# HGRN2 scores on one core: short distances and the diagonal through quarters of the array's columns

## The chip, the cores and the metric

The kernel runs on one core of a Trainium2 chip. The metric is device time of one execution in microseconds (us), as the median of several runs; a profile of one execution shows where it went.

## The reference, cut to what matters

One decoder layer over 1024 tokens of width 1024, in float32: a mixer with two parallel groups (HGRN2, a gated linear recurrence with 4 heads of 128, and a gated short convolution), then a gated MLP. Only the recurrence matters here. For each head, in chunks of tokens:

```python
b = jnp.cumsum(gc, axis=-2)                            # gc = log of the forget gate f
diff = b[..., :, None, :] - b[..., None, :, :]
decay = jnp.exp(jnp.where(causal[:, :, None], diff, -jnp.inf))
scores = jnp.einsum('bhtk,bhsk,bhtsk->bhts', qc, kc, decay)
o = (jnp.einsum('bhts,bhsv->bhtv', scores, vc)
     + jnp.einsum('bhtk,bhkv->bhtv', qc * jnp.exp(b), state))
state = exp(b_last) * state + jnp.einsum('bhsk,bhsv->bhkv', kc * jnp.exp(b_last - b), vc)
```

The decay differs for every channel k, so a score of two tokens is a sum over channels of q, k and the product of the gates between them.

## The kernel before

The tokens are worked in two halves (hf 0 and 1) of 512, each of 4 chunks of 128 (C). Projections, the output projection and the MLP are done as three float32r matmuls for each product (high by high, high by low, low by high): L181 to L183 and L186 to L188, tiles p_q, p_f, p_i, p_g (queries, gates, values, output gates), p_gc, p_ch, p_gb (convolution), p_wo (output projection) and later those of the MLP. They are TensorE's main stream, with 512 moving columns each.

Scores are plain float32 matmuls and are built by distance. UW holds, for 8 pairs of head and chunk (4 heads, 2 chunks of each parity), keys and queries of even and odd chunks as four blocks K, Q, K, Q. F holds the gates. For a chunk, a score of tokens whose positions first part at a block of h tokens belongs to level h (LEVELS, 1 to 64), and the diagonal stands for itself.

- products and diag: kq is the elementwise product of keys and queries, split into kqh and kql; a matmul with ones_r sums it over channels in all 128 rows of sd, and a masked copy (m_diag) puts the diagonal into S.
- level(li): 8 pairs by 2 halves of the chunk's tokens (`tile_position=(0, w * W)`, W = 64), a stationary operand of 64 columns of lhs and 64 moving columns of UW. Then two updates multiply the gates into UW (L389 the left factors, L391 the right ones, so that the next level finds the products over twice the distance), L393 combines the gates in F, and masked copies (m_lev, L399) or, for h = 64, plain copies (L403) put the scores sl into S.
- prepare(li): ScalarE gathers the left factors into lhs, which has one buffer (L371).
- The scores of odd chunks come out transposed: S is copied to odd and even (L443, L444), odd is transposed (so), and copied back.
- chunk_steps: for each chunk output (kt, o), state (st) and finish (mt), with the state carried from chunk to chunk.

These steps wait in a queue named fill. The projections call tick() at set places (the tuples named rate, rates and conv_rates), and each tick takes the next step from the queue, so a step's matmuls stand as a burst between projection matmuls. The steps of the residual and its norm (scale, residual, normalize) go through the same queue in the second half. Weights arrive by SyncE's queue into three buffers and are split on ScalarE (L119) and VectorE (L120).

Of the kernel before, what the change touches and what calls it, by code (L numbers as in the profile page):

```python
# [17 lines left out]
P = 128  # L18
# [5 lines left out]
H = 4  # L24
# [14 lines left out]
G = 2  # L39
GH = G * H  # L40
W = C // 2
N_MASK = C + W * (len(LEVELS) - 1)


@with_exitstack
def decoder_kernel(ctx: ExitStack, tc: tile.TileContext, x, xT, w_sq, w_cv, w_out, w_up, w_dn,
# [24 lines left out]
    m_lev = zp.tile([P, len(LEVELS) - 1, 2, W // 2, GH], U8, name="m_lev")  # L71
# [6 lines left out]
    ones_r = zp.tile([P, P], F32R, name="ones_r")  # L78
    nc.vector.tensor_copy(ones_r[:], ones[:])
# [159 lines left out]
    S = zt("S", (P, 2, C, GH))  # L239
# [56 lines left out]

    def evac_f(hf, pss, rb):
# [3 lines left out]
        kv = UW.rearrange("p (x s) (g j) t -> p x s g j t", x=2, j=H)[:, :, 0]  # L301
        for j, ps in enumerate(pss):
            t = cv(f"tf{hf}_{j}")
            nc.vector.tensor_tensor(t[:], ps[:], rb[:], ALU.mult)
            tv = t.rearrange("p (g x t) -> p x g t", g=2, x=2)
            fj, kj = Fv[:, :, :, j, :], kv[:, :, :, j, :]
            nc.scalar.activation(fj, tv, AF.Sigmoid)
            nc.scalar.activation(kj, tv, AF.Sigmoid, scale=-1.0)
            nc.vector.tensor_scalar(fj, fj, oml[:, j : j + 1], lb[:, j : j + 1], ALU.mult, ALU.add)
            nc.vector.tensor_scalar(kj, kj, oml[:, j : j + 1], None, ALU.mult)  # L310
        return F, UW

    def evac_q(hf, pss, rb, UW):
        nc.scalar.activation(warm, UW[:, 2, 7, 0:1], AF.Silu)
        qv = UW.rearrange("p (x s) (g j) t -> p x s g j t", x=2, j=H)[:, :, 1]
# [23 lines left out]
    def score_steps(hf, F, UW):  # L339
        kq = {}  # L340

        def products(xi, g):
            gs = slice(g * H, (g + 1) * H)
            p = cv(f"kq{hf}_{xi}_{g}", shape=(P, C, H))
            nc.vector.tensor_tensor(
                p.rearrange("p t i -> p i t"), UW[:, 2 * xi, gs, :], UW[:, 2 * xi + 1, gs, :], ALU.mult)
# [3 lines left out]
            kq[xi, g] = hi, lo  # L350

        def diag(xi, g):
            gs = slice(g * H, (g + 1) * H)
            hi, lo = kq[xi, g]
            ps = aux(f"sd{hf}_{xi}_{g}", (P, C, H))
            nc.tensor.matmul(ps[:], ones_r[:], hi[:], start=True, stop=False)
            nc.tensor.matmul(ps[:], ones_r[:], lo[:], start=False, stop=True)
            nc.vector.copy_predicated(S[:, xi, :, gs], m_diag[:].unsqueeze(2).to_broadcast([P, C, H]), ps[:])
            if xi == 1:
                q = UW.rearrange("p (x s) g t -> p x s g t", x=2)[:, :, 1, gs, :]  # L360
                nc.vector.tensor_tensor(q, q, F[:, :, gs, :], ALU.mult)

        def view(t, width, offset, *dims):
            return bass.AP(tensor=t[:].tensor, offset=offset, ap=[[width, P], *[list(d) for d in dims]])
# [3 lines left out]
        def prepare(li):  # L368
            h = LEVELS[li]
            lhss[li] = zt("lhs", (P, GH, C), name=f"lhs{hf}_{li}")  # L370
            nc.scalar.copy(lhss[li].rearrange("p i (b two h) -> p (i b) two h", two=2, h=h),  # L371
                           view(UW, 4 * X, 0, (2 * h, X // (2 * h)), (3 * X + h, 2), (1, h)))

        def level(li):

            h = LEVELS[li]
            n = X // (2 * h)
            ps = aux(f"sl{hf}_{li}", (P, 2, W // 2, GH) if h < W else (P, W, GH))
            lhs = lhss.pop(li)
            halves = [slice(w * W, (w + 1) * W) for w in range(2)]  # L380
            for i in range(GH):
                for w, ws in enumerate(halves):
                    if h < W:
                        rhs = view(UW, 4 * X, X + i * C + w * W + h, (X - h, 2), (2 * h, W // (2 * h)), (1, h))
                    else:
                        rhs = view(UW, 4 * X, X + i * C + (h, X)[w], (1, h))
                    nc.tensor.matmul(ps[ws, ..., i], lhs[:, i, ws], rhs, start=True, stop=True, tile_position=(0, w * W))
            u = view(UW, 4 * X, 0, (3 * X + h, 2), (2 * h, n), (1, h))
            nc.vector.tensor_tensor(u, u, view(F, 2 * X, h, (X - h, 2), (2 * h, n), (0, h)), ALU.mult)  # L389
            w = view(UW, 4 * X, X + h, (X - h, 2), (2 * h, n), (1, h))  # L390
            nc.vector.tensor_tensor(w, w, view(F, 2 * X, 0, (X + h, 2), (2 * h, n), (0, h)), ALU.mult)  # L391
            left = view(F, 2 * X, 0, (X, 2), (2 * h, n))
            nc.vector.tensor_tensor(left, left, view(F, 2 * X, h, (X, 2), (2 * h, n)), ALU.mult)  # L393
            for w, ws in enumerate(halves):
                if h < W:
                    sv = S[ws]
                    to = bass.AP(tensor=sv.tensor, offset=sv.offset + (w * W + h) * GH,
                                 ap=[list(sv.ap[0]), [X - h * GH, 2], [2 * h * GH, W // (2 * h)], [1, h * GH]])
                    nc.vector.copy_predicated(  # L399
                        to, m_lev[ws, li].rearrange("p x (b h) i -> p x b (h i)", h=h),  # L400
                        ps[ws].rearrange("p x (b h) i -> p x b (h i)", h=h))
                else:
                    nc.scalar.copy(S[ws, w, (1 - w) * W : (2 - w) * W], ps[ws])  # L403
# [7 lines left out]
        xg = [(xi, g) for g in range(2) for xi in range(2)]  # L411

        steps = [chain((products, *xg[0]))] + [chain()] * (2 * hf)
        for i in range(4):
            steps.append(chain((diag, *xg[i]), *([(products, *xg[i + 1])] if i < 3 else []),
                               *([(prepare, 0)] if i == 3 else [])))
        for li in range(len(LEVELS)):
            steps.append(chain((level, li), *([(prepare, li + 1)] if li + 1 < len(LEVELS) else [])))
        return steps
# [4 lines left out]
    def chunk_steps(hf, F, UW, v, gg, ma):  # L424
        ma_hi, ma_lo = ma
        shared = {}

        def make(c):
# [4 lines left out]
            K, Q = UW[:, 2 * xi], UW[:, 2 * xi + 1]  # L433
# [3 lines left out]
            def scores():  # L437

                if c == 1:
                    shared["even"] = zt("lhs", (P, GH, C), name=f"even{hf}")  # L440
                    for gi in range(G):
                        shared[gi] = cv(f"odd{hf}_{gi}", shape=(P, H, C))
                        nc.scalar.copy(shared[gi].rearrange("p i t -> p t i"), S[:, 1, :, gi * H : (gi + 1) * H])  # L443
                    nc.scalar.copy(shared["even"].rearrange("p i t -> p t i"), S[:, 0])  # L444
                ps = aux(f"so{n}", (P, H, C))
                for j in range(H):
                    nc.tensor.transpose(ps[:, j, :], shared[g][:, j], ident[:])
                odd = S[:, 1].rearrange("p t i -> p (t i)").rearrange("p (i t) -> p i t", t=C)
                shared["odd"] = odd
                nc.scalar.copy(odd[:, g * H : (g + 1) * H], ps[:])  # L450

            def output():
# [8 lines left out]
                for _, ph, js in hs:  # L461
                    if not first:
                        nc.tensor.matmul(po[:, js], Q[:, ph, :], st[0][:, js], start=True, stop=False)
                    nc.tensor.matmul(po[:, js], shared[("even", "odd")[xi]][:, ph, :], v[c][:, js], start=first, stop=True)
# [87 lines left out]
    def out_proj(hf, mix, gain, hooks=None):  # L552
# [46 lines left out]
        for nh in range(2):  # L599
            if nh and hf:  # L600
                for c in range(NC_H):
# [3 lines left out]
                            hooks=hooks if nh == 0 else None, rate=(2, 2, 1, 1) if hf + nh == 0 else 1)  # L605
# [82 lines left out]
    nc.sync.dma_start(mf[:], masks_d)  # L688
    nc.gpsimd.tensor_copy(m_diag[:], mf[:, :C])
    mv = mf[:, C:].rearrange("p (l x n) -> p l x n", x=2, n=W // 2)  # L690
    for l in range(len(LEVELS) - 1):
# [15 lines left out]
    mix_a = mixers(0, act_a, F0, UW0, rb0, rq0, r0, ma_tiles(0), (1, (1, 1, 1, 2)), (1, 1, 1, 2, 1, 2, 1, 2, 1, 2, 2, 2),  # L707
# [14 lines left out]
    mix_b = mixers(1, act_b, F1, UW1, rb1, rq1, r1, ma_tiles(1), (1, 2), (1, 2, 1, 1, 2, 1, 1, 2, 1, 1, 2, 1))  # L722
# [447 lines left out]
def _masks():  # L1170

    p = np.arange(C)[:, None]
    t = p // W * W + np.arange(W)
    m = [np.eye(C)]
    for h in LEVELS[:-1]:
        same = p // (2 * h) == t // (2 * h)
        left_p, left_t = (p // h) % 2 == 0, (t[0] // h) % 2 == 0
# [53 lines left out]
```

## Time and profile before

| | |
|---|---|
| median of 3 runs | 1100.7 us (1100.54 to 1100.79) |
| the profiled execution | 1099.83 us, its span 1098.0 us |
| level bursts (tile sl) | 14, of 32 records each, from 85.4 to 306.7 us |
| diagonal (tile sd) | 8 times 2 matmuls, from 61.6 to 257.7 us |
| transposes of odd scores (so) | from 126.9 to 345.8 us |

Times in rows are microseconds from the start of the span, or nanoseconds where a row gives min, median and max. PE is TensorE, DVE VectorE, ACT ScalarE. A matmul's record overlaps the next one's, so the spacing of starts tells what one costs in a stream. Each float32 matmul stands as two records; "x32" counts records.

### The profile page before, as it was taken

What the parts mean: (1) busy time and instruction counts of PE and PEld (TensorE: products, weight loads), DVE (VectorE), ACT (ScalarE), POOL (GpSimd) and SP (SyncE); (2) the same over time, 40 slices, a digit from 0 to 9 for tenths busy, and PEclk for the clock granted to TensorE, in tenths of its full rate; (3) what the DMA queues carried; (4) which work ended last, traced back from release to release, by engine and by line L of the source; (5) the groups of instructions that cost most, each with busy time, mean ns of one, the idle gap of its engine ahead of it and who ended that gap; (6) DMA issues with size and microseconds to landing.
All of it is one profiled execution on the core that took longest, in us unless ns stands there. A gap on an engine that the chain in (4) does not pass through costs nothing.

```text
span 1098.0 us, 13874 instructions
## 1 busy us (share of the span) xinstructions
PE 1087.5 (99%) x5312; PEld 900.7 (82%) x5312; DVE 821.5 (75%) x1150; ACT 521.3 (47%) x765; POOL 13.5 (1%) x24
## 2 busy tenths in 40 slices
PE   9999999999999999999999999999999999999996
PEld 7888888888788888888888888888888888888885
DVE  7567977466965675487789888889888767855886
ACT  5543545433454336466445454544454444544541
POOL 2000000000000001000000000000000000000000
PEclk9999999999999999999999999999999999999999
DMA  8522223432352356175243433343332479776632
GB/s 295 190 96 77 81 74 121 138 96 81 116 169 97 106 171 222 66 237 187 85 163 115 153 115 144 125 163 138 130 134 73 155 259 407 304 260 228 209 109 104
DMA packets 56018, 170.14 MB, mean 155 GB/s; under 512 B 5640, under 2 KB 6160, under 8 KB 53008
## 3 DMA queue, kind: packets, MB, share of 16 engines
q1 hardware_dynamic: 54736, 165.24, 43.2%
q0 software_dynamic: 912, 3.67, 1.0%
q8 instruction: 41, 0.67, 0.2%
q10 hardware_dynamic: 304, 0.35, 0.1%
q14 instruction: 25, 0.20, 0.1%
HBM read 133.84 MB, written 35.39 MB: 154 GB/s over the span
## 4 chain that ended last, share of the span: by engine, by line
PE 96%; DVE 3%; issue 0%; ACT 0%; DMA 0%; DVEq 0%; SPq 0%; ACTq 0%
PE pG L181 7%; PE pG L183 7%; PE pG L182 7%; PE pV L181 4%; PE pV L183 4%; PE pV L182 4%; PE pX L188 3%; PE pX L186 3%; PE pX L187 3%; PE pY L186 3%; PE pY L187 3%; PE pY L188 3%; PE p_wo L186 3%; PE p_wo L188 2%; PE p_wo L187 2%; PE pA L183 2%
## 5 line engine op out<-in xcount | busy, mean ns | idle before, releaser
L120 DVE TENSOR_TENSOR ls<-s,hs 128x1024 fp32r<-128x1024 f32 (+1 forms) x40 | 45.2, 1130 | 46.3 <-ACT hs L119 44.4
L119 ACT CAST hs<-s 128x1024 fp32r<-128x1024 f32 (+1 forms) x40 | 39.1, 976 | 78.7 <-PE pY L187 29.9
L796 DVE TENSOR_TENSOR l_t<-t,h_t 128x1536 fp32r<-128x1536 f32 x22 | 38.6, 1755 | 32.6 <-ACT h_t L795 32.6
L795 ACT CAST h_t<-t 128x1536 fp32r<-128x1536 f32 x22 | 32.6, 1484 | 55.2 <-PE pG L182 55.2
L895 ACT ACTIVATE g<-g 128x1024 f32<-128x1024 f32 x22 | 23.4, 1062 | 64.8 <-DVE g L883 64.8
L188 PE MATMUL pY<-hw,ls 128*128 128x512 f32 x132 | 51.4, 390 | 0.0
L187 PE MATMUL pY<-lw,hs 128*128 128x512 f32 x132 | 51.4, 389 | 0.0
L186 PE MATMUL pY<-hw,hs 128*128 128x512 f32 x132 | 51.3, 390 | 0.0
L186 PE MATMUL pX<-hw,hs 128*128 128x512 f32 x116 | 45.2, 390 | 0.0
L187 PE MATMUL pX<-lw,hs 128*128 128x512 f32 x116 | 45.2, 390 | 0.0
L188 PE MATMUL pX<-hw,ls 128*128 128x512 f32 x116 | 45.2, 390 | 0.0
L881 ACT ACTIVATE g<-pG,vec 128x1024 f32<-128x1024 f32 x22 | 24.5, 1114 | 29.0 <-PE pG L183 29.0
L182 PE MATMUL pG<-ulo,h_x 128*128 128x512 f32 x96 | 37.4, 390 | 0.0
L183 PE MATMUL pG<-uhi,l_x 128*128 128x512 f32 x96 | 37.4, 390 | 0.0
L181 PE MATMUL pG<-uhi,h_x 128*128 128x512 f32 x96 | 37.4, 389 | 0.0
L882 DVE SCALAR_TENSOR_TENSOR g<-pG,vec,g 128x1023 f32<-128x1023 f32 x22 | 28.2, 1280 | 8.8 <-ACT g L881 8.3
L181 PE MATMUL pG<-c4h,h_b 128*128 128x512 f32 x88 | 34.4, 390 | 0.0
L182 PE MATMUL pG<-c4l,h_b 128*128 128x512 f32 x88 | 34.3, 390 | 0.0
L183 PE MATMUL pG<-c4h,l_b 128*128 128x512 f32 x88 | 34.3, 390 | 0.0
L181 PE MATMUL pV<-c3h,h_b 128*128 128x512 f32 x88 | 34.3, 390 | 0.0
L183 PE MATMUL pV<-c1h,l_t 128*128 128x512 f32 x88 | 34.3, 390 | 0.0
L181 PE MATMUL pG<-c2h,h_t 128*128 128x512 f32 x88 | 34.3, 390 | 0.0
(366 smaller groups left out, 3362.8 us busy)
## 6 DMA issues: line engine op xcount, KB each, us to landing
w<-w_up SPq DMA_DIRECT2D x21, 1024.0 KB, 4.8
b<-w_dn SPq DMA_DIRECT2D x35, 512.0 KB, 7.8
s<-s_d SPq DMA_DIRECT2D x33, 512.0 KB, 4.7
s_d<-g SPq DMA_DIRECT2D x22, 512.0 KB, 2.7
s_d<-S SPq DMA_DIRECT2D x11, 768.0 KB, 3.5
r_wo<-w_out SPq DMA_DIRECT2D x16, 512.0 KB, 3.5
ah_w<-w_up SPq DMA_DIRECT2D x10, 512.0 KB, 4.5
f_d<-ah_f SPq DMA_DIRECT2D x9, 512.0 KB, 3.0
```

The costliest lines, as they stand in the source:

```text
L119: nc.scalar.copy(hi, src)
L120: nc.vector.tensor_tensor(lo, src, hi.bitcast(F32), ALU.subtract)
L181: nc.tensor.matmul(ps, whi, ahi, start=first, stop=False, skip_group_check=more)
L182: nc.tensor.matmul(ps, whi, alo, start=False, stop=False, skip_group_check=more)
L183: return nc.tensor.matmul(ps, wlo, ahi, start=False, stop=last, skip_group_check=more)
L186: nc.tensor.matmul(ps, ahi, whi, start=first, stop=False, skip_group_check=more)
L187: nc.tensor.matmul(ps, ahi, wlo, start=False, stop=False, skip_group_check=more)
L188: return nc.tensor.matmul(ps, alo, whi, start=False, stop=last, skip_group_check=more)
L795: m = nc.scalar.copy(hi[:], src)
L796: casts[name] = m.ins, nc.vector.tensor_tensor(lo[:], src, hi[:].bitcast(F32), ALU.subtract).ins
L881: nc.scalar.mul(a[:], c, wc[2])
L882: nc.vector.scalar_tensor_tensor(a[:, 1:], c[:, : T - 1], wc[1], a[:, 1:], ALU.mult, ALU.add)
```

## The change

Levels 1 to 32 work on quarters of 32 tokens: 4 matmuls for each of the 8 pairs, with 32 stationary and 32 moving columns, at column positions 0, 32, 64 and 96. Levels 1 to 16 and the diagonal are masked into a small tile near, whose token index counts within 32 tokens, with 5 masks instead of 6; 8 plain copies (put_near) bring it into S, and levels 32 and 64 are copied into S from sl. The diagonal is summed by plain float32 matmuls with a stationary operand of 32 columns of ones, in four column positions, so the split into kqh and kql is gone; products and diag work on 8 pairs at a time. S is kept as pair by token, so the copies odd and even are gone. The blocks of UW lie as K, Q, Q, K, and prepare(li + 1) is called inside level(li), between its two updates. There are two steps fewer in each half's queue; the rates at some places are changed with it.

```diff
-G = 2
-GH = G * H
-W = C // 2
+GH = 2 * H
+W = 32
+LOW = sum(h < W for h in LEVELS)
...
-    ones_r = zp.tile([P, P], F32R, name="ones_r")
-    nc.vector.tensor_copy(ones_r[:], ones[:])
+    near = zp.tile([P, 2, W, GH], F32, name="near")
+    nc.gpsimd.memset(near[:], 0.0)
...
-    S = zt("S", (P, 2, C, GH))
+    S = zt("S", (P, 2, 8, C))
...
+    K_AT, Q_AT = (0, 3), (2, 1)
...
-            nc.scalar.activation(qv[:, :, :, j, :], t.rearrange("p (g x t) -> p x g t", g=2, x=2), AF.Silu)
+            for xi in range(2):
+                nc.scalar.activation(
+                    qv[:, Q_AT[xi], :, j, :], t.rearrange("p (g x t) -> p x g t", g=2, x=2)[:, xi], AF.Silu)
...
-            hi = cv(f"kqh{hf}_{xi}_{g}", F32R, (P, C, H))
-            lo = cv(f"kql{hf}_{xi}_{g}", F32R, (P, C, H))
-            split(p[:], hi[:], lo[:])
...
-            nc.tensor.matmul(ps[:], ones_r[:], hi[:], start=True, stop=False)
-            nc.tensor.matmul(ps[:], ones_r[:], lo[:], start=False, stop=True)
-            nc.vector.copy_predicated(S[:, xi, :, gs], m_diag[:].unsqueeze(2).to_broadcast([P, C, H]), ps[:])
...
+        def diag(xi):
+            ps = aux(f"sd{hf}_{xi}", (P, GH, W))
+            for g in range(2):
+                for q in range(C // W):
+                    ws = slice(q * W, (q + 1) * W)
+                    nc.tensor.matmul(ps[ws, g * H : (g + 1) * H], ones[:, :W], kq[xi, g][:, :, ws], start=True, stop=True,
+                                     tile_position=(0, q * W))
+            nc.vector.copy_predicated(near[:, xi], m_diag[:, :W].unsqueeze(2).to_broadcast([P, W, GH]),
+                                      ps.rearrange("p i t -> p t i"))
...
-                           view(UW, 4 * X, 0, (2 * h, X // (2 * h)), (3 * X + h, 2), (1, h)))
+                           view(UW, 4 * X, 0, (2 * h, X // (2 * h)), (X + h, 2), (1, h)))
...
-            halves = [slice(w * W, (w + 1) * W) for w in range(2)]
+            low, wide = h < W, max(h, W)
+            parts = [slice(t, t + wide) for t in range(0, C, wide)]
             for i in range(GH):
-                for w, ws in enumerate(halves):
+                for q, ws in enumerate(parts):
...
-                    nc.tensor.matmul(ps[ws, ..., i], lhs[:, i, ws], rhs, start=True, stop=True, tile_position=(0, w * W))
-            u = view(UW, 4 * X, 0, (3 * X + h, 2), (2 * h, n), (1, h))
+                    nc.tensor.matmul(ps[ws, ..., i], lhs[:, i, ws], rhs, start=True, stop=True, tile_position=(0, ws.start))
+            u = view(UW, 4 * X, 0, (X + h, 2), (2 * h, n), (1, h))
             nc.vector.tensor_tensor(u, u, view(F, 2 * X, h, (X - h, 2), (2 * h, n), (0, h)), ALU.mult)
-            w = view(UW, 4 * X, X + h, (X - h, 2), (2 * h, n), (1, h))
+            if li + 1 < len(LEVELS):
+                prepare(li + 1)
+            w = view(UW, 4 * X, 2 * X + h, (X - h, 2), (2 * h, n), (1, h))
...
+        def put_near(xi):
+            for t in range(0, C, W):
+                ws = slice(t, t + W)
+                nc.scalar.copy(S[ws, xi, :, ws], near[ws, xi].rearrange("p t i -> p i t"))
...
-                        nc.scalar.copy(shared[gi].rearrange("p i t -> p t i"), S[:, 1, :, gi * H : (gi + 1) * H])
-                    nc.scalar.copy(shared["even"].rearrange("p i t -> p t i"), S[:, 0])
...
-                            hooks=hooks if nh == 0 else None, rate=(2, 2, 1, 1) if hf + nh == 0 else 1)
+                            hooks=hooks if nh == 0 else None, rate=(2, 1, 1, 1) if hf + nh == 0 else 1)
...
-    mix_a = mixers(0, act_a, F0, UW0, rb0, rq0, r0, ma_tiles(0), (1, (1, 1, 1, 2)), (1, 1, 1, 2, 1, 2, 1, 2, 1, 2, 2, 2),
+    mix_a = mixers(0, act_a, F0, UW0, rb0, rq0, r0, ma_tiles(0), (1, 1), (1, 1, 1, 2, 1, 1, 2, 1, 1, 2, 2, 1),
...
-    mix_b = mixers(1, act_b, F1, UW1, rb1, rq1, r1, ma_tiles(1), (1, 2), (1, 2, 1, 1, 2, 1, 1, 2, 1, 1, 2, 1))
+    mix_b = mixers(1, act_b, F1, UW1, rb1, rq1, r1, ma_tiles(1), ((1, 1, 1, 2), 2), (1, 2, 1, 1, 2, 1, 1, 2, 1, 1, 2, 1))
```

Two places of TensorE's order show what moves. The first is the burst of level 0 in the first half; sl is its result, p_g the projection of output gates, p_i that of values. Before:

```order
L186 MATMUL p_g_3_705<-h_g_1_744,hi_3_206 128x512
L187 MATMUL p_g_3_705<-l_g_1_745,hi_3_206 128x512
L188 MATMUL p_g_3_705<-h_g_1_744,lo_3_207 128x512
L387 MATMUL sl_0_773<-UW_392,lhs_0_741 64x64 x16
L186 MATMUL p_g_0_702<-h_g_2_798,hi_4_236 128x512
L187 MATMUL p_g_0_702<-l_g_2_799,hi_4_236 128x512
L188 MATMUL p_g_0_702<-h_g_2_798,lo_4_237 128x512
L186 MATMUL p_g_0_702<-h_g_2_798,hi_5_257 128x512
```

and in the changed kernel:

```order
L186 MATMUL p_i_3_539<-h_i_3_663,hi_7_308 128x512
L187 MATMUL p_i_3_539<-l_i_3_664,hi_7_308 128x512
L188 MATMUL p_i_3_539<-h_i_3_663,lo_7_309 128x512
L391 MATMUL sl_0_692<-UW_392,lhs_0_660 32x32 x32
L186 MATMUL p_g_0_739<-h_g_0_744,hi_0_135 128x512
L187 MATMUL p_g_0_739<-l_g_0_745,hi_0_135 128x512
L188 MATMUL p_g_0_739<-h_g_0_744,lo_0_136 128x512
```

The burst has 32 matmuls of 32 columns instead of 16 of 64, and it stands two ticks earlier, between the last matmul of the values and the first of the gates.

The second place is level 3 of the second half, behind the output projection of the first half (p_wo). Before:

```order
L186 MATMUL p_i_0_2454<-h_i_1_2513,hi_3_1710 128x512
L387 MATMUL sl_3_2488<-UW_1886,lhs_3_2438 64x64 x9
L186 MATMUL p_i_3_2457<-h_i_0_2459,hi_0_1692 128x512
L187 MATMUL p_i_3_2457<-l_i_0_2460,hi_0_1692 128x512
L188 MATMUL p_i_3_2457<-h_i_0_2459,lo_0_1693 128x512
L186 MATMUL p_i_3_2457<-h_i_0_2459,hi_1_1698 128x512
L187 MATMUL p_i_3_2457<-l_i_0_2460,hi_1_1698 128x512
L188 MATMUL p_i_3_2457<-h_i_0_2459,lo_1_1699 128x512
L387 MATMUL sl_3_2488<-UW_1886,lhs_3_2438 64x64 x7
L187 MATMUL p_i_0_2454<-l_i_1_2514,hi_3_1710 128x512
```

and in the changed kernel:

```order
L186 MATMUL p_wo_1_3_2321<-h_wo_1_3_2532,mah_534 128x512
L187 MATMUL p_wo_1_3_2321<-l_wo_1_3_2533,mah_534 128x512
L188 MATMUL p_wo_1_3_2321<-h_wo_1_3_2532,mal_535 128x512
L391 MATMUL sl_3_2563<-UW_1972,lhs_3_2526 32x32 x32
L186 MATMUL p_i_0_2616<-h_i_0_2621,hi_0_1778 128x512
L187 MATMUL p_i_0_2616<-l_i_0_2622,hi_0_1778 128x512
L188 MATMUL p_i_0_2616<-h_i_0_2621,lo_0_1779 128x512
L186 MATMUL p_i_0_2616<-h_i_0_2621,hi_1_1784 128x512
```

The burst stood in two pieces, 9 and 7 matmuls, among the projection of values with a part of another of its rows drawn in between; now it is one piece of 32, directly behind the output projection.

More of the change, by code (lines that the diff above doesn't have):

```diff
@@ L38 @@
 V_N = V_FCONV + 3 * 2 * NF
-G = 2
-GH = G * H
-W = C // 2
-N_MASK = C + W * (len(LEVELS) - 1)
+GH = 2 * H
+W = 32
+LOW = sum(h < W for h in LEVELS)
+N_MASK = W * (1 + LOW)
 @with_exitstack
@@ L70, in decoder_kernel @@
     m_diag = zp.tile([P, C], U8, name="m_diag")
-    m_lev = zp.tile([P, len(LEVELS) - 1, 2, W // 2, GH], U8, name="m_lev")
+    m_lev = zp.tile([P, LOW, 2, W // 2, GH], U8, name="m_lev")
     conv_halo = zp.tile([P, 4, 2], F32, name="conv_halo")
@@ L409, in chain @@
             return run
[L411 to L419, printed above, removed]
+        steps = [chain((products, 0))] + [chain()] * (2 * hf)
+        steps += [chain((diag, 0), (products, 1)), chain((diag, 1), (prepare, 0))]
+        return steps + [chain((step, li)) for li in range(len(LEVELS))]
     st = [None]
@@ L437, in scores @@
             def scores():
[L439 to L444, printed above, removed]
-                ps = aux(f"so{n}", (P, H, C))
[L446 to L450, printed above, removed]
+                ps = aux(f"so{n}", (P, H, C))
+                for j, ph, _ in hs:
+                    nc.tensor.transpose(ps[:, j, :], S[:, 1, ph, :], ident[:])
+                nc.scalar.copy(S[:, 1, g * H : (g + 1) * H, :], ps[:])
             def output():
@@ L463, in output @@
                         nc.tensor.matmul(po[:, js], Q[:, ph, :], st[0][:, js], start=True, stop=False)
-                    nc.tensor.matmul(po[:, js], shared[("even", "odd")[xi]][:, ph, :], v[c][:, js], start=first, stop=True)
+                    nc.tensor.matmul(po[:, js], S[:, xi, ph, :], v[c][:, js], start=first, stop=True)
                 ssq = small(f"sso{n}")
@@ L687, in decoder_kernel @@
     mf = xslot("mf")
[L688 to L691, printed above, removed]
+    nc.sync.dma_start(mf[:, :N_MASK], masks_d)
+    nc.gpsimd.tensor_copy(m_diag[:, :W], mf[:, :W])
+    mv = mf[:, W:N_MASK].rearrange("p (l x n) -> p l x n", x=2, n=W // 2)
+    for l in range(LOW):
         nc.gpsimd.tensor_copy(m_lev[:, l], mv[:, l].unsqueeze(3).to_broadcast([P, 2, W // 2, GH]))
```

78 lines of the change are left out of this document (39 added, 39 removed).

## The prediction

> **What bounds the kernel now.** I read the page's engine totals first, then the chain that ended last, the order of time on TensorE around the instructions that the change touches, and last the groups and waits of their tiles.
>
> ```profile
> span 1098.0 us, 13874 instructions
> PE 1087.5 (99%) x5312; PEld 900.7 (82%) x5312; DVE 821.5 (75%) x1150; ACT 521.3 (47%) x765; POOL 13.5 (1%) x24
> PEclk9999999999999999999999999999999999999999
> PE 96%; DVE 3%; issue 0%; ACT 0%; DMA 0%; DVEq 0%; SPq 0%; ACTq 0%
> ```
>
> TensorE is busy 99% of the span at the full granted clock, and 96% of the chain that ended last is TensorE. So a change pays only by what it takes from TensorE's own row of matmuls, or from the few tenths of a microsecond where that row has a gap. The question is what one burst of score matmuls costs there. Rows in order of time, of TensorE alone (start us, us, then the operation):
>
> ```profile
> 85.07 0.39 PE L188 MATMUL p_g<-h_g,lo 128*128 128x512 f32 x1
> 85.39 1.16 PE L387 MATMUL sl<-UW,lhs 128*64 128x64 f32 x32
> 86.48 0.50 PE L186 MATMUL p_g<-h_g,hi 128*128 128x512 f32 x1
> 86.82 0.40 PE L187 MATMUL p_g<-l_g,hi 128*128 128x512 f32 x1
> 87.05 0.39 PE L188 MATMUL p_g<-h_g,lo 128*128 128x512 f32 x1
> 126.89 0.39 PE L183 MATMUL p_gc<-hi,l_gc 128*128 128x512 f32 x1
> 127.12 1.09 PE L447 MATMUL so<-ident,odd 128*128 128x128 f32 x8
> 127.97 0.48 PE L181 MATMUL p_ch<-hi,h_ch 128*128 128x512 f32 x1
> ```
>
> Projection matmuls start 0.23 us apart (86.82 to 87.05). Every float32 matmul of the scores stands as two records (16 in the program, x32 here). One level of distances delays the projection by 86.82 - 85.07 = 1.75 us less two normal steps, 1.75 - 0.45 = **1.30 us**. There are 14 such bursts (7 levels, two halves), some 18 us, all on the path.
>
> A second place shows gaps, in the second half of the tokens, where a burst waits and the next comes in two pieces:
>
> ```profile
> 276.92 0.39 PE L188 MATMUL p_wo<-h_wo,mal 128*128 128x512 f32 x1
> 277.66 1.15 PE L387 MATMUL sl<-UW,lhs 128*64 128x64 f32 x32 [0.35 <-ACT lhs L371]
> 283.65 0.39 PE L186 MATMUL p_i<-h_i,hi 128*128 128x512 f32 x1
> 284.13 0.80 PE L387 MATMUL sl<-UW,lhs 128*64 128x64 f32 x18
> 285.34 0.50 PE L186 MATMUL p_i<-h_i,hi 128*128 128x512 f32 x1 [0.42 <-DVE m_o L550]
> 286.92 0.68 PE L387 MATMUL sl<-UW,lhs 128*64 128x64 f32 x14
> ```
>
> **The change part by part.** *Levels 1 to 32 through quarters of the columns.* A level had 8 heads x 2 halves of the columns; it gets 8 heads x 4 quarters, each with 32 moving columns instead of 64. Twelve bursts change; the two of level 64 keep their form.
>
> What is one step worth? In the piece of 18 records one half works through 10 and the other through 8; the piece of 14 has 8 at most on a half, the whole burst of 32 has 16. So (1.16 - 0.68) / (16 - 8) = **0.060 us for one step**, and both halves take that step together: 32 records of 0.060 one after the other would be 1.9 us. A record of the same kind with 128 moving columns takes (127.97 - 127.12) / 8 = 0.106 us alone. A straight line through 64 columns (0.060) and 128 columns (0.106) gives 0.037 us for 32 columns. Strict proportion to 64 columns gives 0.030 us. No shrinking at all gives 0.060. And quarters that can't be fed together give more (the rival below). I take 0.037, since both of its rows are float32 records of this kind and the second half joined the first at no cost: the last two steps of the piece of 18 are one half alone, and its length (0.80 against 0.68 for two steps fewer) has the same 0.060 per step. What isn't steps in a burst, 1.30 - 16 x 0.060 = 0.34 us, is entry and exit (85.07 to 85.39 is 0.32, not 0.23; 86.48 to 86.82 is 0.34), and stays.
>
> So a level goes from 1.30 to 0.34 + 16 x 0.037 = 0.93 us; 12 x 0.37 = **-4.4 us** (-5.8 at 0.030, 0 at 0.060).
>
> The Trainium skill has a rule against this: "TensorE: Matmul & The Clock Gate", section "Wait — 56ns, not 53.3ns?", says that matmuls of one kind don't start closer than about 25 ns however few their columns (with 32 columns 25 ns, against 13.3 ns of array time), and "TensorEngine Tiling (Array Packing)", section "Instruction Overhead", says not to take the tiling from a dimension that is already small. If each record here pays that floor twice, an estimate from that page is 0.050 us a step; the level term is then -1.9 us and the time 1097.0 us. No row of before has fewer than 64 moving columns on half an array, so the trace doesn't decide it.
>
> *Diagonal.* Before, each of 8 products went through two full-array matmuls:
>
> ```profile
> 61.34 0.40 PE L188 MATMUL p_i<-h_i,lo 128*128 128x512 f32 x1
> 61.58 0.40 PE L356 MATMUL sd<-kqh,ones_r 128*128 128x512 f32 x1
> 61.81 0.39 PE L357 MATMUL sd<-kql,ones_r 128*128 128x512 f32 x1
> 62.04 0.40 PE L186 MATMUL p_i<-h_i,hi 128*128 128x512 f32 x1
> ```
>
> That is 62.04 - 61.58 = 0.46 us each with no entry or exit cost, 3.7 us in all. Now there are 4 bursts of 8 float32 matmuls (16 records) in four quarters, so 4 steps of 128 columns at 0.106, plus 0.34 for entry and exit: 0.76 each, 3.1 us in all: **-0.6 us**. If the quarters don't overlap, 16 x 0.106 + 0.34 = 2.0 us each, +4.4.
>
> *Copies of the left factor, and the regrouping.* Keys and queries of the two parities lay as K, Q, K, Q; now they lie as K, Q, Q, K, so that the left factors of all levels are one half of the tile and the right factors the other; and the copy for the next level is issued ahead of the second update instead of behind it. What it is worth is read from the waits of the copies (tile lhs; engine awaited, us, times):
>
> ```profile
> L371 ACT COPY lhs<-UW x14: 1037/1054/1527, 67.1 to 302.7; 128x1024 f32<-128x1024 f32 x14
>   DVE UW L391: 21.2, 7
>   ACT lhs L371: 4.1, 10
> L389 DVE TENSOR_TENSOR UW<-UW,F x14: 1211/1219/1226, 87.7 to 304.2; 128x1024 f32<-128x1024 f32 x14
> L391 DVE TENSOR_TENSOR UW<-UW,F x14: 1199/1206/1220, 89.5 to 307.4; 128x1024 f32<-128x1024 f32 x14
> ```
>
> In the long way round (burst, first update 1.2 us, mask copy, second update 1.2 us, copy 1.05 us, next burst) the copy waited 21.2 us for the second update, though that update writes only right factors. With the halves apart, the copy needs the first update and the end of the burst, no more. TensorE itself lost little to this, and only in the second half: burst 2 starts 0.74 us after the last projection matmul instead of 0.32 (+0.42); burst 3 starts 0.48 after it (+0.16), TensorE idles 0.42 us behind its first piece, and the second piece pays 0.34 us of entry and exit again. Together 1.3 us. In the new order burst 3 is one piece and its successors lie 24 projection matmuls apart, 24 x 0.23 = 5.5 us, against 1.05 us for the copy and about 3 us for what VectorE does ahead of the second update there (four evacuations of p_wo, L550, at 0.65 us by rows below). I take 1.0 us of the 1.3 as gone: **-1.0 us** (ends: -1.3, and +1.0 if the evacuations push the second update past the next burst twice as far as now).
>
> ```profile
> 277.86 1.29 DVE L550 TENSOR_TENSOR m_o<-p_wo,pg 128x512 f32<-128x512 f32 x2
> 279.81 1.22 DVE L389 TENSOR_TENSOR UW<-UW,F 128x1024 f32<-128x1024 f32 x1
> 283.03 1.05 ACT L371 COPY lhs<-UW 128x1024 f32<-128x1024 f32 x1 [3.90 <-DVE rt_m L165]
> ```
>
> *VectorE and ScalarE work.* The rows for what goes:
>
> ```profile
> L399 DVE COPY_PREDICATED S<-m_lev,sl x24: 698/734/751, 88.9 to 303.5; 64x512 f32<-64x512 uint8 x24
> L403 ACT COPY S<-sl x4: 562/574/585, 122.3 to 307.7; 64x512 f32<-64x512 f32 x4
> L358 DVE COPY_PREDICATED S<-m_diag,sd x8: 714/720/723, 62.3 to 258.4; 128x512 f32<-128x512 uint8 x8
> L345 DVE TENSOR_TENSOR kq<-UW x8: 1060/1065/1082, 54.9 to 243.0; 128x512 f32<-128x512 f32 x8
> L119 ACT CAST kqh<-kq x8: 613/620/624, 56.0 to 247.8; 128x512 fp32r<-128x512 f32 x8
> L120 DVE TENSOR_TENSOR kql<-kq,kqh x8: 684/686/694, 56.6 to 249.0; 128x512 fp32r<-128x512 f32 x8
> L443 ACT COPY odd<-S x4: 1143/1178/1195, 125.3 to 336.1; 128x512 f32<-128x512 f32 x4
> L444 ACT COPY even<-S x2: 2065/2083/2101, 123.5 to 311.1; 128x1024 f32<-128x1024 f32 x2
> ```
>
> VectorE loses 24 x 0.73 + 8 x 0.72 + 8 x 0.69 = 28.8 us, and 8 products get cheaper (1.07 with a strided result; 0.69 is the row nearest to a packed one, 3.0 us); it gains 14 masked copies of 256 elements (estimate 0.4 each by half of the 512 and a fixed part, 5.6 us): about -26 of 821 us. ScalarE loses 8 x 0.62 + 4 x 1.18 + 2 x 2.08 = 13.8 us and gains 24 copies of 32 x 256 (estimate 0.4 each from the 64x512 row, 9.6 us) and 8 more starts of the query activation: about -3 us. None of this is on the path: it lies beside the projection matmuls, 5.5 us of TensorE between two bursts, in which VectorE is busy 75% on average. If that cover were gone in one gap, a copy of 1.05 us late would cost TensorE the part by which it is late, as in the row at 277.66. The cast of ones, the masks' smaller load and the new clearing on GpSimd lie in the first microseconds, before the scores begin at 61 us; zero. On the queues, some weight loads follow a row or residual transfer that they preceded; every weight load has three buffers ahead of it, zero.
>
> *Chunk steps.* Their matmuls are the same, but they come in 2 bursts fewer. Leaving a burst costs 128.28 - 127.97 = 0.31 against 0.23 us by the step after the row at 127.97: **-0.2 us**.
>
> ```profile
> 128.28 0.39 PE L182 MATMUL p_ch<-lo,h_ch 128*128 128x512 f32 x1
> ```
>
> **Sum.** -4.4 - 0.6 - 1.0 - 0.2 = **-6.2 us**. The profiled execution took 1099.8 us (span 1098.0 and 1.8 around it), 0.9 below the median of 1100.7. Its own time becomes 1093.6, and the median with the same distance 1094.5 us.
>
> **The rivals.**
>
> *A step does not shrink below that of 64 columns* (0.060 us with 32 as with 64). For it: the rows hold no shorter step, and entry and exit show that something besides columns is paid. Against: 128 to 64 columns did shrink it from 0.106 to 0.060, near proportion. Then levels bring nothing; diagonal, gaps and chunk steps bring 0.6 + 1.0 + 0.2 = 1.8: 1098.9 us. The page's floor of 0.050 lies between this and the forecast (1097.0 as above).
>
> *The array is not fed with twice as many records* (ends on the other side). Each changed burst issues 64 records and 64 weight loads instead of 32 and 32. Before, a burst got 32 records in 16 x 0.060 = 0.96 us, 0.030 each. If that is the pace at which TensorE's queue can be refilled, and not the columns' time, 64 records take 1.92 us: +0.96 x 12 = +11.5 us, with the other terms -1.8 unchanged, 1110.4 us. It decides the sign when a record costs more than (0.96 + 1.8 / 12) / 64 = 0.017 us. For it: no row of before shows a pace under 0.030 per record over a whole burst. Against: a half alone has the same 0.060 per step as two halves together, so the columns' time explains the pace with nothing left over.
>
> *The gaps in the second half stay or grow*, since the level bursts move to where the residual's evacuations stand on VectorE: +1.0 instead of -1.0, 1096.5 us; inside the range.
>
> **How the numbers follow.** The time can be told from no change from about 0.2% on, 2.2 us. The forecast (a step between 0.030 and 0.045) gets 0.58; a floor near 0.050 to 0.060 gets 0.24, about half of it beyond 2.2 us faster; quarters that aren't fed, 0.18, nearly all of it slower. Faster 0.70, same 0.12, slower 0.18. The forecast's own range is 1092.8 (step 0.030, all gaps gone) to 1096.5 (step 0.037, gaps grown). The range with the floor cases in it is 1092 to 1100.5; it leaves out the slow rival and little else.
>
> **What would show it.** In the changed kernel the burst of 64 records of level 0 should be busy about 0.8 us instead of 1.16, and the second projection matmul behind it should start 1.4 us after the last one ahead instead of 1.75. The diagonal's 16 records should take some 0.6 us. The copy of lhs should no longer wait for the second update of UW, and the bursts of the second half should start 0.32 us behind their projection matmul. A busy time of a burst above 1.3 us, or a TensorE total that does not fall below 1085 us, would show the forecast wrong.

## The result and the profile after

The changed kernel takes 1093.62 us in the median (1093.01 to 1095.54, 6 runs) against 1100.62 us before: the ratio is 0.9939, 95% interval 0.9926 to 0.9952, so 7 us and 0.6% faster. The prediction was 1094.5 us, range 1092 to 1100.5.

The page of the changed kernel, span and engine totals:

```profile
span 1093.7 us, 14738 instructions
PE 1082.3 (99%) x5744; PEld 894.9 (82%) x5744; DVE 794.2 (73%) x1123; ACT 522.9 (48%) x783; POOL 11.3 (1%) x24
```

TensorE is the bound as before. It has 432 records more and is busy 5.2 us less. VectorE lost 27 us (26 were forecast), which no run shows in the time by itself. ScalarE, forecast at 3 us less, has 1.6 us more (521.3 to 522.9): its copies out of near take 0.69 us each (16, median) where 0.4 was estimated; the 8 out of sl at level 32 take 0.37.

The profiled execution of the changed kernel took 1095.54 us, 1.9 us above its median, because its first projection matmuls ran slowly; the last section shows it. So bursts are compared below, not spans.

TensorE in order of time around one diagonal burst, the burst of level 0, and the burst of level 3 in the second half:

```profile
63.69 0.39 PE L188 MATMUL p_i<-h_i,lo 128*128 128x512 f32 x1
64.01 0.64 PE L359 MATMUL sd<-kq,ones 128*32 128x128 f32 x16
64.58 0.50 PE L186 MATMUL p_i<-h_i,hi 128*128 128x512 f32 x1
64.92 0.40 PE L187 MATMUL p_i<-l_i,hi 128*128 128x512 f32 x1
...
76.25 0.39 PE L188 MATMUL p_i<-h_i,lo 128*128 128x512 f32 x1
76.57 0.76 PE L391 MATMUL sl<-UW,lhs 128*32 128x32 f32 x64
77.26 0.51 PE L186 MATMUL p_g<-h_g,hi 128*128 128x512 f32 x1
77.60 0.40 PE L187 MATMUL p_g<-l_g,hi 128*128 128x512 f32 x1
78.08 0.40 PE L186 MATMUL p_g<-h_g,hi 128*128 128x512 f32 x1
...
276.61 0.39 PE L188 MATMUL p_wo<-h_wo,mal 128*128 128x512 f32 x1
276.93 0.76 PE L391 MATMUL sl<-UW,lhs 128*32 128x32 f32 x64
```

A level delays the projection by 77.60 - 76.25 - 0.45 = 0.90 us, by the measure that gave 1.30 before. The next two starts behind it are 0.03 wider than usual (0.48 against 0.45; before, 0.46): counted in, 0.93 us instead of 1.31. A diagonal burst costs 64.92 - 63.69 - 0.45 = 0.78 us. Level 3 of the second half is one piece and starts 0.32 us behind the last matmul of p_wo, like a burst that waits for nothing.

The copies lhs in the changed kernel: their row, then the only row of their list of waits that names an engine (us in total, times), then a row of VectorE's waits (us in total, times, us of the longest):

```profile
L373 ACT COPY lhs<-UW x14: 1037/1048/1537, 62.0 to 294.4; 128x1024 f32<-128x1024 f32 x14
  DVE UW L366: 2.2, 1
DVE UW L397 <- PE sl L391: 14.6, 7, 4.7
```

The copy no longer waits for the second update (L366 stands ahead of the levels); that update, L397, now waits for the burst, which reads the right factors that it overwrites.

### The profile page after: what moved, and what is told of

Same layout as the page of the kernel before. It is cut to its first block, busy times and chain, and to the rows that moved or that the text cites. A ratio compares the mean times of both kernels' runs of the same rounds, so it can differ in the third digit from the quotient of the medians.

```text
span 1093.7 us, 14738 instructions
## 1 busy us (share of the span) xinstructions
PE 1082.3 (99%) x5744; PEld 894.9 (82%) x5744; DVE 794.2 (73%) x1123; ACT 522.9 (48%) x783; POOL 11.3 (1%) x24
## 4 chain that ended last, share of the span: by engine, by line
PE 97%; DVE 2%; DMA 0%; issue 0%; ACT 0%; DVEq 0%; SPq 0%; ACTq 0%
PE pG L183 7%; PE pG L181 7%; PE pG L182 7%; PE pV L183 4%; PE pV L181 4%; PE pV L182 4%; PE p_wo L186 3%; PE pX L187 3%; PE pX L188 3%; PE pX L186 3%; PE p_wo L187 3%; PE p_wo L188 3%; PE pY L186 3%; PE pY L187 3%; PE pY L188 3%; PE pA L183 2%
## 5 line engine op out<-in xcount | busy, mean ns | idle before, releaser
L182 PE MATMUL pG<-c7l,h_t 128*128 128x512 f32 x88 | 34.3, 389 | 0.0
```

Source lines behind the costliest of these rows:

```text
L182: nc.tensor.matmul(ps, whi, alo, start=False, stop=False, skip_group_check=more)
```

## The experiments

**The regrouping alone, in the kernel before.**

```diff
+    K_AT, Q_AT = (0, 3), (2, 1)
...
+            if li + 1 < len(LEVELS):
+                prepare(li + 1)
-            w = view(UW, 4 * X, X + h, (X - h, 2), (2 * h, n), (1, h))
+            w = view(UW, 4 * X, 2 * X + h, (X - h, 2), (2 * h, n), (1, h))
```

> The kernel before with the regrouping alone: blocks of UW as K, Q, Q, K and the copy for the next level ahead of the second update; levels still in halves of 64 columns, diagonal still through the whole array. If the quarters carry the gain, a level burst keeps its 1.30 us and only the gaps of the second half go: 1.0 to 1.5 us faster than before, 1099.1 to 1099.6 us. Rival, the shorter way round carries the gain: 5 us or more faster, 1095 us or below.

Measured 1099.13 us against 1100.13, ratio 0.9990 (0.9981 to 0.9999). TensorE in the second half:

```profile
276.64 0.39 PE L188 MATMUL p_wo<-h_wo,mal 128*128 128x512 f32 x1
276.96 1.15 PE L391 MATMUL sl<-UW,lhs 128*64 128x64 f32 x32
280.87 0.39 PE L188 MATMUL p_i<-h_i,lo 128*128 128x512 f32 x1
281.19 1.15 PE L391 MATMUL sl<-UW,lhs 128*64 128x64 f32 x32
283.11 0.50 PE L186 MATMUL p_i<-h_i,hi 128*128 128x512 f32 x1 [0.34 <-DVE m_o L556]
```

Both bursts start 0.32 us behind their projection matmul and come in one piece, but they stand closer together, and the projection behind them waits for an evacuation instead. So the regrouping by itself is worth about 1 us (0.1 to 2.1 by the interval), and the bursts keep their 1.15 us. The rival in which it carries the gain is out.

**The two loops of a level exchanged, in the changed kernel.**

```diff
-            for i in range(GH):
-                for q, ws in enumerate(parts):
+            for q, ws in enumerate(parts):
+                for i in range(GH):
```

> The changed kernel with the two loops of a level exchanged: all 8 pairs of one quarter first, then the next quarter. Same matmuls, same data, other order. If the gain comes from four quarters working at once, and that needs matmuls of different quarters next to each other, a level burst takes 64 steps of 0.035 us instead of 16, 1.7 us longer, 12 times: some 20 us slower than the changed kernel, 1113 us. Rival, a record of 32 columns is simply short (0.57 us / 64 = 0.009 us) whatever its neighbours: no change, 1093.6 us.

Measured 1108.41 us (ratio to before 1.0072, 1.0053 to 1.0090), 14.8 us slower than the changed kernel. The burst of level 0 and that of level 64, which is still in halves:

```profile
74.35 1.92 PE L391 MATMUL sl<-UW,lhs 128*32 128x32 f32 x64
76.20 0.50 PE L186 MATMUL p_g<-h_g,hi 128*128 128x512 f32 x1
119.41 1.90 PE L391 MATMUL sl<-UW,lhs 128*64 128x64 f32 x32
121.23 0.50 PE L181 MATMUL p_gb<-hi,h_gb 128*128 128x512 f32 x1
```

From its first start to the next projection matmul the level takes 1.85 us instead of 0.69 (77.26 - 76.57). Twelve times 1.16, and twice 0.74 for level 64 (1.82 against 1.08), is 15.4 us. So the gain is the work of quarters at the same time, and it needs matmuls of different quarters next to each other in the order.

How far they work at the same time shows in single starts. A window of 0.005 us lists the records under way in it, from the first one's start to the last one's end. First a half alone (this run, at 119.80), then two halves together (the changed kernel, at 115.55), then a quarter alone (this run, at 74.66):

```profile
119.63 0.40 PE L391 MATMUL sl<-UW,lhs 128*64 128x64 f32 x4
115.34 0.40 PE L391 MATMUL sl<-UW,lhs 128*64 128x64 f32 x8
74.47 0.39 PE L391 MATMUL sl<-UW,lhs 128*32 128x32 f32 x7
```

Two halves have twice the records under way in the same 0.40 us, so the second half joins at no cost; starts in one half lie 0.058 us apart either way. In a quarter alone they lie 0.031 us apart (the median), somewhat less than the 0.035 of the expectation. Where one quarter follows another in the order, the starts of the two mix (0.002 to 0.008 us apart), which brings the mean of the burst down to 0.027 us and, with it, this run's loss below the 20 us expected. Four quarters together take 0.57 us from the first start to the last, 0.57 / 16 = 0.036 for a step: 4 x 0.031 / 0.036 = 3.4 times as fast as one quarter by steps, 1.85 / 0.69 = 2.7 times by whole bursts. The Trainium skill, "TensorEngine Tiling (Array Packing)", section "Theoretical Speedup", gives up to 4 times for dimensions up to 32; the trace stays under that.

**Half the moving columns.** In levels 1 to 16, with 16 instead of 32.

```diff
-                        rhs = view(UW, 4 * X, 2 * X + i * C + ws.start + h, (X - h, 2), (2 * h, W // (2 * h)), (1, h))
+                        rhs = view(UW, 4 * X, 2 * X + i * C + ws.start + h, (2 * h, W // (2 * h)), (1, h))
...
```

> The changed kernel with 16 moving columns instead of 32 in levels 1 to 16: it leaves out the scores of odd chunks at these distances. If a step goes on shrinking with its columns, on the line through 0.060 (64) and 0.035 (32) to some 0.023 us, ten bursts lose 16 x 0.012 us each: 1.9 us faster than the changed kernel. Rival, 0.035 us is already a floor (four records with their weight loads take that long to issue, or 32 stationary columns to load): a burst stays at 0.57 us from first to last start, no change in time.

Measured 1093.13 us (ratio to before 0.9932, 0.9917 to 0.9947): no difference from the changed kernel that this can tell.

```profile
74.66 0.74 PE L391 MATMUL sl<-UW,lhs 128*32 128x16 f32 x64
75.32 0.49 PE L186 MATMUL p_g<-h_g,hi 128*128 128x512 f32 x1
```

The burst takes 0.66 us to the next projection matmul instead of 0.69, with half the columns. The mean step is 0.035 us against 0.036, so moving columns hardly set it any more. The prediction's line through 128 and 64 columns does not go on below 32.

**Half the stationary columns too.** 16 by 16 in the same levels; the masked copies are split to match.

```diff
-                    nc.tensor.matmul(ps[ws, 0, :, i] if low else ps[ws, ..., i], lhs[:, i, ws], rhs,
+                    hs = slice(ws.start, ws.start + W // 2)
+                    nc.tensor.matmul(ps[hs, 0, :, i] if low else ps[ws, ..., i], lhs[:, i, hs if low else ws], rhs,
...
```

> The changed kernel with 16 stationary and 16 moving columns for each matmul of levels 1 to 16: it leaves out three quarters of the scores at these distances. It asks what holds a step of four quarters at 0.035 us when 16 moving columns didn't shorten it. If it is the load of 32 stationary columns (0.027 us by a quarter alone), the step falls to some 0.020 us and ten bursts to 0.33 us from first to last start. Rival, it is the pace at which records and their loads are issued (4 x 0.009): the burst stays at 0.55 us.

```profile
74.34 0.70 PE L392 MATMUL sl<-UW,lhs 128*16 128x16 f32 x64
74.97 0.50 PE L186 MATMUL p_g<-h_g,hi 128*128 128x512 f32 x1
```

0.63 us, against 0.66 and 0.69: with a quarter of the work the burst is 9% shorter. Where it is shorter shows in the records under way early and late in this burst, at 74.55 and at 74.80:

```profile
74.38 0.35 PE L392 MATMUL sl<-UW,lhs 128*16 128x16 f32 x28
74.62 0.35 PE L392 MATMUL sl<-UW,lhs 128*16 128x16 f32 x22
```

A record takes 0.176 us here. So early a record starts every (0.35 - 0.176) / 27 = 0.0064 us, 0.026 for a step of four, and late every (0.35 - 0.176) / 21 = 0.0083 us, 0.033 for a step. By the single starts, the second to the eighth step take 0.032 us in the changed kernel, 0.032 with half the moving columns and 0.025 here; the last five take 0.033 to 0.034 in all three (medians). Between them lie one or two longer steps, up to 0.067 us. So early in a burst the step goes with the stationary columns, and four quarters together take hardly longer for it than one quarter alone (0.031); late in it the columns make no difference. What is left there is the number of records, 0.0083 us for each with its weight load. That the pace of issue is the cause is an inference from what is left over; no run shows the issue by itself, or why it sets in only halfway. The run's time, 1093.8 us, holds a new wait of 0.9 us in one burst that came in two pieces, for an evacuation behind the split masked copies on VectorE, and is not compared.

**16 by 16, one quarter after the other** (the edits of the exchanged loops and of the last experiment together).

> The kernel with 16 stationary and 16 moving columns, one quarter after the other (loops exchanged). With 32 columns a quarter alone took 0.027 us a record. If that was columns or loads, it falls to about 0.014 us and a burst of 64 records to 0.9 us. Rival, a quarter can't start records closer than a floor of about 0.025 us however few the columns: 64 records still take 1.6 to 1.7 us.

```profile
76.13 1.52 PE L392 MATMUL sl<-UW,lhs 128*16 128x16 f32 x64
77.58 0.50 PE L186 MATMUL p_g<-h_g,hi 128*128 128x512 f32 x1
```

1.45 us to the next projection matmul, between the two expectations. The records under way at 76.40, all of one quarter:

```profile
76.24 0.33 PE L392 MATMUL sl<-UW,lhs 128*16 128x16 f32 x7
```

That is (0.33 - 0.176) / 6 = 0.026 us for a record, and by the single starts 41 of the burst's 63 gaps are exactly 0.025 us. Where one quarter follows another the starts of the two mix (0.005 and 0.02 us apart); that alone keeps the burst below the 1.6 us of the rival. So the rival held: half the columns bring a quarter from 0.031 only to 0.025 us, not to 0.014. This is the floor of about 25 ns between matmuls that the Trainium skill states ("TensorE: Matmul & The Clock Gate", section "Wait — 56ns, not 53.3ns?"); the trace agrees within a quarter. It does not hold across quarters: four together start a record every 0.009 us (0.57 / 63) in the changed kernel. The prediction let a step pay that floor twice (0.050 us, 1097.0 us). A step has one record of each quarter, so it pays once, and with 32 columns a quarter's own 0.031 us is above it; the measurement decides against 1097.0 us.

**The diagonal through the whole array again, in the changed kernel.**

```diff
...
-                    nc.tensor.matmul(ps[ws, g * H : (g + 1) * H], ones[:, :W], kq[xi, g][:, :, ws], start=True, stop=True,
-                                     tile_position=(0, q * W))
...
+                nc.tensor.matmul(ps[:], ones_r[:], hi[:], start=True, stop=False)
+                nc.tensor.matmul(ps[:], ones_r[:], lo[:], start=False, stop=True)
...
```

> The changed kernel with the diagonal through the whole array again (products split in two, two matmuls of 128x512 for each, as before), the levels in quarters. If the prediction's term is right, each of 4 diagonal steps costs 4 x 0.23 = 0.92 us instead of 0.84: 0.3 us (by the bursts measured) to 0.6 us (as predicted) slower than the changed kernel, 1093.9 to 1094.2 us. Rival, the added splits and masked copies on VectorE make TensorE wait: 1 us or more slower.

Measured 1095.71 us (ratio to before 0.9961, 0.9947 to 0.9974), about 2 us slower than the changed kernel and more than the bursts explain: the three diagonal steps without a wait delay the projection by 0.95 us each against 0.78, 0.7 us for four. TensorE in the second half:

```profile
252.10 0.40 PE L365 MATMUL sd<-kql,ones_r 128*128 128x512 f32 x1
253.05 0.50 PE L188 MATMUL p_wo<-h_wo,mbh 128*128 128x512 f32 x1 [0.55 <-DVE m_o L562]
```

And from TensorE's waits (engine and what it was to work on, what it waited for: us in total, times, us of the longest):

```profile
PE p_wo L188 <- DVE m_o L562: 1.0, 2, 0.6
```

TensorE waits twice, 1.0 us in all, for evacuations that VectorE brings late. So the rival came true in this kernel. But ahead of the first of these evacuations VectorE works through two splits (0.69 us each) and through 8 masked copies (2.43 us), which stand here in the place of one of 0.45, since the diagonal has to land in the small tile. So the run doesn't tell whether the splits alone would make TensorE wait, and no value of VectorE's relief is shown.

**The regrouping undone, in the changed kernel.** Blocks as K, Q, K, Q, and the copy for the next level behind the mask copy.

```diff
-    K_AT, Q_AT = (0, 3), (2, 1)
+    K_AT, Q_AT = (0, 2), (1, 3)
...
-            if li + 1 < len(LEVELS):
-                prepare(li + 1)
...
-        return steps + [chain((step, li)) for li in range(len(LEVELS))]
+        return steps + [chain((step, li), *([(prepare, li + 1)] if li + 1 < len(LEVELS) else [])) for li in range(len(LEVELS))]
```

> The changed kernel with the regrouping undone: blocks of UW as K, Q, K, Q, and the copy for the next level behind the second update and the mask copy. The bursts keep their 0.57 us; what comes back is waiting. If the prediction's term of 1.0 us for the regrouping holds in the changed kernel too, 1.0 to 1.5 us slower than it, with bursts of the second half starting late behind their projection matmul. Rival, the bursts lie 24 projection matmuls apart now, which is enough for the long way round as well: no change, 1093.5 us.

Measured 1095.53 us (ratio to before 0.9963, 0.9951 to 0.9976), some 2 us slower than the changed kernel. All but one of the bursts start 0.32 us behind their projection matmul. TensorE at the place of that one:

```profile
295.53 0.39 PE L188 MATMUL p_i<-h_i,lo 128*128 128x512 f32 x1
297.70 1.15 PE L391 MATMUL sl<-UW,lhs 128*64 128x64 f32 x32 [1.78 <-ACT lhs L373]
```

ScalarE up to that burst's copy lhs:

```profile
288.67 4.23 ACT L414 COPY S<-near 32x256 f32<-32x256 f32 x6
294.49 1.48 ACT L408 COPY S<-sl 32x256 f32<-32x256 f32 x4
296.62 1.03 ACT L373 COPY lhs<-UW 128x1024 f32<-128x1024 f32 x1
```

The same place of ScalarE in the changed kernel:

```profile
294.38 1.04 ACT L373 COPY lhs<-UW 128x1024 f32<-128x1024 f32 x1
295.33 1.48 ACT L410 COPY S<-sl 32x256 f32<-32x256 f32 x4
```

Level 64 of the second half starts 2.17 us behind its projection matmul instead of 0.32: 1.85 us, nearly the whole difference. Behind the copies out of near its copy lhs stands in both kernels; here it stands behind the plain copies of level 32 (1.48 us) and an activation as well, in the changed kernel ahead of them. VectorE's second update had ended long before (292.80), so this is not the wait that the prediction spoke of. The trace speaks for the place of the call as the cause; the layout was undone with it, and the two were not told apart by a run.

**Both diagonal bursts directly ahead of level 0.** A kernel that might beat both, from the 0.37 us of entry and exit (0.93 - 16 x 0.035).

```diff
...
-        steps += [chain((diag, 0), (products, 1)), chain((diag, 1), (prepare, 0))]
-        return steps + [chain((step, li)) for li in range(len(LEVELS))]
+        steps += [chain((products, 1)), chain((queries,), (prepare, 0))]
+        return steps + [chain(*([(diag, 0), (diag, 1)] if li == 0 else []), (step, li)) for li in range(len(LEVELS))]
```

Here queries is the update of the queries that stood in diag.

> The changed kernel with both diagonal bursts put directly ahead of level 0 in one step, so that three bursts of each half enter and leave the quarters once instead of three times. If 0.37 us of entry and exit is charged for each visit to the quarters, four visits fewer bring 1.5 us: 1092.1 us. Rival, it is charged for each change of the form of matmul (128 moving columns to 32), or the later diagonal puts a wait somewhere: no change or slower, 1093.6 us or more.

Measured 1092.07 us (ratio to before 0.9928, 0.9915 to 0.9940). Rows of TensorE, the last one the second projection matmul behind the bursts:

```profile
72.30 0.39 PE L188 MATMUL p_i<-h_i,lo 128*128 128x512 f32 x1
72.62 1.08 PE L359 MATMUL sd<-kq,ones 128*32 128x128 f32 x32
73.52 0.77 PE L392 MATMUL sl<-UW,lhs 128*32 128x32 f32 x64
74.56 0.40 PE L187 MATMUL p_g<-l_g,hi 128*128 128x512 f32 x1
```

The three bursts delay the projection by 74.56 - 72.30 - 0.45 = 1.81 us, against 0.78 + 0.78 + 0.90 = 2.46 apart: 0.65 us in each half, 1.3 in all. The step from the diagonal to the level costs nothing that shows (72.62 + 8 steps of 0.11 is 73.50), so entry and exit belong to a visit to the quarters.

To have it beside the changed kernel on the same chip, both ran once more:

> The changed kernel once more, beside the merged one on the same chip: 1093.0 to 1093.6 us where the first weights come early, 0.993 to 0.995 of the kernel before.

> The merged kernel (both diagonal bursts directly ahead of level 0) beside the changed one on the same chip. Its bursts were 1.5 us shorter in the trace, so 1.5 us faster than the changed kernel if nothing waits for it. Rival: equal within 0.3 us, the earlier difference came from the chip or the start.

Measured 1093.59 us for the changed kernel (ratio to before 0.9941, 0.9928 to 0.9953) and 1091.78 us for the merged one (0.9918, 0.9905 to 0.9932): 1.8 us by the medians, in the sense forecast. The two intervals overlap a little, so the size stays open; the 1.3 us that the bursts lost agree with it. It is the fastest kernel of this study.

## Why the prediction was right, point by point

- *Levels, -4.4 us.* 0.93 us for each was forecast and 0.90 measured by the same measure, 12 x 0.40 = -4.8 us (0.93 against 1.31, -4.6, with the wider starts behind a burst); exchanging the loops lost it and more. The reason given was half wrong. 0.037 us was taken from a line in the number of moving columns, and the mean step, 0.036, lies close to it. But it is a mean of early steps of 0.032, which go with the stationary columns, of a few long ones, and of late steps of 0.034, on which columns have no effect. That these meet the line is luck. With 16 moving columns the line gives 0.026 us and the run 0.035.
- *The half that joined at no cost.* Right: 0.058 us a step alone and together. It spoke for the 0.037 and against the slow rival.
- *Diagonal, -0.6 us.* 0.78 us measured for 0.76. The term is 4 x 0.78 against 8 x 0.46, -0.6 us; put back, the bursts cost 0.7 us. Its effect through VectorE, taken as zero, was not told: the kernel with the diagonal put back waits 1.0 us for VectorE, with masked copies that neither kernel has.
- *Regrouping and gaps, -1.0 us.* All of the 1.3 us went, so the term was sized 0.3 too small. The mechanism held where the regrouping was put in alone, about 1 us, though one wait of 0.34 us for VectorE stayed there that the changed kernel doesn't have. Undone, it cost about 2 us, but for a reason not forecast: a copy lhs late behind ScalarE's other copies, which also took longer than forecast (out of near 4.23 / 6, about 0.7 us each, for 0.4).
- *Chunk steps, -0.2 us.* Not tested by a run of its own.
- *The sum* of these readings is -4.8 - 0.6 - 1.3 - 0.2 = -6.9 us; measured is -7.0, between -5.3 and -8.1 by the interval. So most of the 0.8 us that the forecast of -6.2 lacked is in the levels (0.4) and the gaps (0.3), both sized too small. The signs named came too: the burst of level 0 is busy 0.76 us, the diagonal's 0.64, and TensorE's total is 1082.3 us.
- *The rivals.* The step did shrink. The slow rival, TensorE not fed with twice the records, is out: 64 records take 0.69 us, 0.011 each, below the 0.017 from which it would have decided. Its thought was sound, though: late in a burst the number of records, 0.0083 us each, is all that is left to set the step.

## What to carry to other kernels

Where the main stream is TensorE's, read what a small burst costs from the start ahead to the second start behind it, and split it into steps and a fixed part: the two call for different remedies (more tiles at once, fewer visits). Column tiles paid here only where matmuls of different tiles stand next to each other in the order, and below 32 columns smaller matmuls brought almost nothing, so look for fewer of them instead. Look at single starts inside a burst before dividing its length by a count: here the mean mixed two paces and a few long steps. When an engine off the path is relieved, look where it had been late; when small copies are added to it, look at what is queued behind them.

## What the runs showed of the hardware that was not expected

Fewer columns than 32 by 32 bring four quarters almost nothing (0.69, 0.66, 0.63 us for 64 records), while one quarter alone still gains (1.85 to 1.45 us). For about half a burst, four quarters together step as fast as one alone (0.032 for 0.031 us; with 16 columns both 0.025); then the step is 0.033 to 0.034 whatever the columns.

The start of an execution can cost 2 us. In these windows (stretch, its length, busy time of TensorE, weight loads, VectorE, ScalarE and GpSimd, then the granted clock, DMA share and GB/s), first of the changed kernel and then of the kernel before:

```profile
6.00:10.40 4.40, 3.97 (x10) 2.95 (x11) 4.40 (x10) 3.55 (x7) 0.00 (x0) 0.65 1.04 387
```

```profile
6.00:10.40 4.40, 4.32 (x20) 3.55 (x20) 4.40 (x10) 3.90 (x8) 0.00 (x0) 1.00 1.06 394
```

In the profiled execution of the changed kernel TensorE idled 1.33 us before its first projection matmul, the granted clock then was 0.65 on average over 4.4 us, and it did 10 matmuls where the other did 20:

```profile
5.98 0.47 PE L181 MATMUL p_f<-hi,h_f 128*128 128x512 f32 x1 [1.33 <-ACT acc L264]
8.42 0.63 PE L181 MATMUL p_f<-hi,h_f 128*128 128x512 f32 x1
8.85 0.63 PE L182 MATMUL p_f<-lo,h_f 128*128 128x512 f32 x1
```

These start 0.43 us apart, where 0.23 is usual. Ten matmuls of 0.23 us are 2.3 us, which is about what this execution lies above the lower ones of the same kernel (1095.54 against 1093.0 to 1093.6). The idle time does not explain it. In the second run of the merged kernel TensorE waited less than 0.1 us for its first projection matmul, and its matmuls then started 0.43 us apart as well (rows below); in the run with half the moving columns it idled 0.46 and 0.42 us and they started 0.23 apart (7.17 to 7.40).

```profile
7.25 0.63 PE L181 MATMUL p_f<-hi,h_f 128*128 128x512 f32 x1
7.68 0.63 PE L182 MATMUL p_f<-lo,h_f 128*128 128x512 f32 x1
```

Six of the twelve profiled executions began in this way, and in five of them the row of the granted clock reads 1.00 over the same stretch. So the spacing of matmuls shows it where the clock's row doesn't; what sets it off stays open.
